# Gate stage of a streaming-encoder layer: the last 128 tokens with tokens on partitions

## The chip, the cores and the metric

The kernel runs on one core of one Trainium2 chip. The metric is the device time of one execution in microseconds (us). Times are from the program's start on the device to its end; the profile shows one execution, whose span (first to last instruction) is a little shorter than its time.

The engines are TensorE (PE; its weight loads are shown as PEld), VectorE (DVE), ScalarE (ACT), GpSimd (POOL) and SyncE (SP, which issues transfers here). PE multiplies a stationary operand (128 x 128) with a moving one (128 x up to 512 columns) and writes to PSUM, which has 8 banks of 512 columns.

## The reference, cut to what matters

One layer on 1024 tokens of width 1024: a mixer with attention, a gated MLP, and then the stage that the change touches, which takes a per-layer input embedding `p`, gates it, and adds it; a final norm closes the trunk.

```python
def rmsnorm(x, g):
    xf = x.astype(jnp.float32)
    y = xf * lax.rsqrt(jnp.mean(xf * xf, axis=-1, keepdims=True) + EPS)
    return (y * g.astype(jnp.float32)).astype(x.dtype)
...
    hn = rmsnorm(h, norm_ple_g[i])
    gate = jax.nn.sigmoid(hn @ w_ple_gate[i] + b_ple_gate[i])
    h = h + gate * (p[i] @ w_ple[i])
return rmsnorm(h, final_g)
```

`w_ple_gate` is 1024 x 1024, `p` is 1024 x 256, `w_ple` is 256 x 1024.

## The kernel before, in words

Everything is held transposed: features on the 128 partitions, tokens along the columns. The residual h is `H[d]`, d = 0 to 7 for the eight groups of 128 features, each with 1024 token columns. fp32 products are made of three products of reduced-precision halves: an operand is split into hi and lo, and `mm3` (L128) multiplies hi x hi (L130), hi x lo (L131) and lo x hi (L132). So each step over 128 features of the contraction is three matmuls.

The gate stage is a list of items (L1186). An item (d, a, b) is the feature group d for tokens a to b. Each takes `gate_mm` (8 steps over the contraction, 24 matmuls; the weights `wg` are stationary, the normalised residual `hp` is moving) and `ple_mm` (2 steps, 6 matmuls; `wp` stationary, `pt` moving). The items run in this order: eight with tokens 0 to 511, six with tokens 512 to 1023 (d = 0 to 5), and then d = 6 and 7 for tokens 512 to 767 and again for 768 to 1023. The gate products go to PSUM banks 2, 3 and 7 in turn, the ple products to 5 and 6. The loop issues the gate products of an item, then the ple products of the same item (L1205), and `gate_out` for it.

`gate_out` (L1148) is, for the second half: sigmoid on ACT (L1154), gate times ple product on DVE (L1155), residual added on DVE (L1156). Then the final norm: `Norm.add` squares the new residual on ACT (L645, L647) and adds it up over the feature groups on DVE (L649), and ACT scales the residual by the final gain (L1209).

When the last group of a token range is in, `Norm.sums` (L652) adds over the partitions with matmuls against a column of ones (L655, L657), one per 128 tokens, DVE scales (L658), and POOL raises to the power -1/2 (L659). `Norm.rows` (L661) spreads 1/rms over the partitions by a transpose on PE per 128 tokens (L663). `emit` (L1168) multiplies the residual by it on DVE (L1173) and issues the output transfers (L1174), in turn on SP's and ACT's queue. For tokens 512 to 767 the sums stand behind the gate products of the second last item and the rows in the middle of the last item's; for tokens 768 to 1023 both stand behind the last item.

PE's instructions run in the order in which the code is written (`manual_schedule`); on the other engines a scheduler orders them by their dependences and the place in the code. Each engine takes its instructions strictly one after another, and a transfer is issued by the queue of the engine that it is written on.

`hp[1]` (tokens 512 to 1023) lies in a region called B, `hp[0]`, `wg`, `pt` and `wp` in regions R0 to R4. Region 2 holds `hp[0]` (tokens 0 to 511) and is not used after item 7.

Of the kernel before, what the change touches and what calls it, by code (L numbers as in the profile page):

```python
# [6 lines left out]
F32 = mybir.dt.float32  # L7
F32R = mybir.dt.float32r
AF = mybir.ActivationFunctionType
ALU = mybir.AluOpType  # L10

P = 128
SEQ = 1024
D = 1024
KT = D // P
# [7 lines left out]
MAX_REL = 128  # L23
WINDOWS = (2, 4, 8, 16)
HIST = 16
EPS = 1e-6
BIG = 3.0e38

# [53 lines left out]


def trunk(tc, xT, pT, vecs, w_qk0, w_in, w_v, bias, counts, pool_w, w_out, w_up, w_down,
          w_gate, w_ple, out):
    nc = tc.nc
    act, dve, pe, pool, sp = nc.scalar, nc.vector, nc.tensor, nc.gpsimd, nc.sync

    with tc.tile_pool(name="sb", bufs=1) as sb, \
# [10 lines left out]
        Rs = [region(z, F32R) for z in range(5)]  # L100
        F = sb.tile([P, 15616], F32, name="F")
        ident = sb.tile([P, P], F32, name="ident")
        vec = sb.tile([P, NVEC], F32, name="vec")
        small = sb.tile([P, 80], F32, name="small")
        PS = pp.tile([P, 8, 512], F32, name="PS")
# [16 lines left out]
        def f(kb, n):  # L122
            return F[:, int(kb * KW):int(kb * KW) + n]
# [15 lines left out]
        mhalf = small[:, 0:1]  # L139
# [27 lines left out]
        qk32 = [f(38 + 4 * s, 1024) for s in range(2)]  # L167
        U = f(38, 4 * (HIST + SEQ)).rearrange("p (g t) -> p g t", g=4)
        T1 = f(54.25, 272)
# [293 lines left out]
        def pool_out(g, q, u, src, eng):  # L463

            win, n, f0 = WINDOWS[g], HIST + 256, HIST
            if q == 0:
# [105 lines left out]
        for i in range(NI + 3):  # L572
            if i >= 7:
                sums_due(i, (i - 6) // 2)
            if i < NI:
                h, t, k0, nk = keys(i)
# [43 lines left out]
        H = [f(8 + 4 * d, 1024) for d in range(KT)]  # L620
# [188 lines left out]
        for z, d in enumerate((0, 4, 1, 5, 2, 6, 3, 7)):  # L809
            k = z // 2  # L810
# [222 lines left out]
        wg = [None] * KT  # L1033
        hp = [None, None]
# [90 lines left out]
        pt = [(r(8 * k, 1024), r(8 * k + 4, 1024)) for k in range(2)]  # L1125
        wp = [(r(16 + 8 * k, 1024), r(20 + 8 * k, 1024)) for k in range(2)]
# [11 lines left out]
        def gate_mm(d, a, b, bank, middle=None):  # L1138
            ds_ = slice(d * P, (d + 1) * P)
            ts_ = slice(a % 512, a % 512 + b - a)  # L1140
            for k in range(KT):
                hi, lo = hp[a // 512][k]
                mm3(PS[:, bank, 0:b - a], wg[k][:, ds_], wg[k][:, 1024:2048][:, ds_], hi[:, ts_], lo[:, ts_],
                    k == 0, k == KT - 1)
                if k == 3 and middle:
                    middle()
# [21 lines left out]
        def emit(norm):  # L1168

            n = 1024 // (norm.nt * P)  # L1170
            for z, d in enumerate(range(0, KT, n)):
                h_ = HH[:, d:d + n, norm.ts]
                dve.tensor_tensor(h_, h_, norm.out.unsqueeze(1).to_broadcast([P, n, norm.nt * P]), ALU.mult)  # L1173
                (sp, act)[z % 2].dma_start(  # L1174
                    out[d * P:(d + n) * P, norm.ts].rearrange("(e p) t -> p e t", p=P), h_)

        zt = [f(2 * s, 512) for s in range(4)]
        acc, sq = f(52.25, 512), f(54.25, 512)
        lasts = {(0, 512): Norm(slice(0, 512), f(40, 512), [f(42, 512)], 4, 1),
                 (512, 1024): Norm(slice(512, 1024), acc, [sq], 4, 1)}  # L1180
        for z, ab in enumerate(((512, 768), (768, 1024))):
            zs = slice(256 * z, 256 * z + 256)
            lasts[ab] = Norm(slice(*ab), acc[:, zs], [sq[:, zs]], 4, z, z == 0)
            lasts[ab].n = 6
        ple_banks, gate_banks = (5, 6), (2, 3, 7)
        items = ([(d, 0, 512) for d in range(KT)] + [(d, 512, 1024) for d in range(6)]  # L1186
                 + [(d, a, a + 256) for a in (512, 768) for d in (6, 7)])

        def ended(ab):
            lasts[ab].rows()  # L1190
            emit(lasts[ab])

        for i, (d, a, b) in enumerate(items):
            gate_mm(d, a, b, gate_banks[i % 3], (lambda: ended((512, 768))) if i == 17 else None)
            if i == 0:
                continue
            if i == 16:
                lasts[512, 768].sums()
            if i == 1:
                norm_b.sums()  # L1200
            if i == 2:
                norm_b.rows(rst2[:, HS[1]])
            for z in ((0, 1) if i == 1 else (i,)):
                dz, az, bz = items[z]
                ple_mm(dz, az, bz, ple_banks[z % 2])  # L1205
                gate_out(dz, az, bz, gate_banks[z % 3], ple_banks[z % 2], zt[z % 4])
                lasts[az, bz].add(dz)
                hz = H[dz][:, az:bz]
                act.activation(hz, hz, AF.Copy, scale=vec[:, C_GL + dz:C_GL + dz + 1])  # L1209
# [12 lines left out]
def _layout(i):

    c = np.ascontiguousarray
    x = i["x"][0]
    w_in = i["w_in"][0]
    w_up = i["w_up"][0]
    d = {}
    d["xT"] = c(x.T).reshape(KT, P, SEQ)
    d["pT"] = c(i["p"][0, 0].T).reshape(2, P, SEQ)  # L1230

    def cols(v, n):
        return np.asarray(v).reshape(n, P).T

    cw = i["conv_w"][0]
    d["vecs"] = c(np.concatenate(
        [cols(i["norm_mix_g"][0], KT)] + [cols(cw[j], NF) for j in range(3)]
        + [cols(i["conv_b"][0], NF), cols(i["pool_b"][0], 4), cols(i["pool_scale"][0], 4)]
        + [cols(i[n], KT) for n in ("norm_ffn_g", "norm_ple_g", "b_ple_gate", "final_g")], axis=1))
    wt = w_in.reshape(KT, P, 16, P).transpose(2, 1, 0, 3)  # L1240
    d["w_qk0"] = c(np.concatenate([wt[4], wt[8]], axis=2)).reshape(P, KT * 2 * P)
    d["w_in"] = c(wt[:12]).reshape(12, P, D)
    d["w_v"] = c(w_in[:, 1536:].reshape(KT, P, 2, 256).transpose(2, 1, 0, 3)).reshape(2, P, KT * 256)
    ii = np.arange(P)[:, None] + 512 - np.arange(BANDT * P)[None, :]
    d["bias"] = c(i["rel_bias"][0][:, np.clip(ii, -MAX_REL, MAX_REL) + MAX_REL])
    d["counts"] = np.tile((1.0 / np.arange(1, 17)).astype(np.float32)[None, :], (P, 1))
    d["pool_w"] = c(i["pool_w"][0].transpose(1, 0, 2)).reshape(P, 512)
    d["w_out"] = c(i["w_out"][0].reshape(8, P, 2, 512).transpose(2, 0, 1, 3))
    d["w_up"] = c(w_up.reshape(KT, P, 2, NF, P).transpose(3, 2, 1, 0, 4)).reshape(NF, 2, P, D)
    d["w_down"] = c(i["w_down"][0].reshape(NF, P, D))  # L1250
    d["w_gate"] = c(i["w_ple_gate"][0].reshape(KT, P, D))
    d["w_ple"] = c(i["w_ple"][0].reshape(2, P, D))
    return d


# [15 lines left out]
```

## Time and profile before

| | us |
|---|---|
| median of 3 runs (lowest, highest) | 1139.93 (1139.84, 1141.75) |
| the profiled execution, its time | 1138.89 |
| the profiled execution, its span | 1137.1 |
| mean granted clock of TensorE | 0.997 |

How to read the rows of a profile: a row of the timeline gives the start and the length in us, the engine, the source line, the operation, output <- inputs by the program's tile names (PS is PSUM, F the working buffer that holds `H`, R and B the operand regions), the shape, and in brackets how long the engine had been idle and who released it. A "128x1 x8" row of L655 is the sums of four token tiles, each recorded as two matmuls. A row of grouped instructions ends with count, total us, mean ns, idle time before them and its releaser. A row of the windows gives a stretch, its length, the busy time of PE, PEld, DVE, ACT and POOL (with instructions started), PE's granted clock, the busy share of the transfer engines and GB/s.

### The profile page before, as it was taken

Reading aid. Unit: us, or ns where it says so; the run is one execution under the profiler, and the core shown is the slowest. Engines: PE = TensorE matmul, PEld = TensorE weight load, DVE = VectorE, ACT = ScalarE, POOL = GpSimd, SP = SyncE. Lnnn points to the kernel's source line nnn. Section 1 sums busy time; section 2 is a strip of 40 time slices with the busy share of each in tenths; the row PEclk is TensorE's granted clock in tenths of the full one; section 3 lists DMA queues with packets and bytes.
Section 4 is the critical chain, followed back from the end, with each engine's and each line's share of the span. In section 5 each row is a group of like instructions: output and inputs, shape, how many; then the busy total and the mean of one; then the engine's idle time right before and its main releaser. Section 6 shows DMA issues by size and latency. Waiting matters only on the chain.

```text
span 1137.1 us, 15326 instructions
## 1 busy us (share of the span) xinstructions
PE 1121.7 (99%) x5517; PEld 944.6 (83%) x5517; DVE 891.4 (78%) x1371; ACT 577.9 (51%) x1001; POOL 281.5 (25%) x297
## 2 busy tenths in 40 slices
PE   9999999999999999999999999999999999999996
PEld 7988998888888878888888888887888888888886
DVE  7678878779656788989898999988896688757344
ACT  8568677765554553434343434344444567545222
POOL 0013334275002213444463555333000000000000
PEclk9999999999999999999999999999999999999998
DMA  7134756534500343142635463414673564310012
GB/s 266 38 86 114 166 118 179 122 85 130 185 14 16 122 156 102 65 140 78 172 100 157 115 167 93 102 37 127 233 269 102 167 193 159 121 48 1 1 74 75
DMA packets 63340, 133.46 MB, mean 117 GB/s; under 512 B 7392, under 2 KB 9696, under 8 KB 62816
## 3 DMA queue, kind: packets, MB, share of 16 engines
q1 hardware_dynamic: 51664, 107.25, 28.5%
q0 software_dynamic: 9856, 23.07, 11.1%
q10 hardware_dynamic: 1744, 2.17, 0.5%
q8 instruction: 43, 0.70, 0.3%
q14 instruction: 33, 0.27, 0.1%
HBM read 116.73 MB, written 45.09 MB: 142 GB/s over the span
## 4 chain that ended last, share of the span: by engine, by line
PE 88%; DVE 6%; ACT 2%; issue 2%; DMA 1%; SPq 0%; DVEq 0%; POOLq 0%; POOL 0%; ACTq 0%
PE PS L130 27%; PE PS L132 27%; PE PS L131 27%; PE PS L370 2%; PE PS L387 1%; PE PS L388 1%; DVE R L136 1%; DVE B L378 1%; ACT F L356 1%; PE PS L344 1%; PE PS L345 1%; DMA F<-in_w_qk 0%; DVE F L346 0%; DMA R<-GD 0%; PE PS L353 0%
## 5 line engine op out<-in xcount | busy, mean ns | idle before, releaser
L130 PE MATMUL PS<-R,R 128*128 128x512 f32 (+1 forms) x932 | 359.7, 386 | 2.7 <-ACT R L135 1.4
L132 PE MATMUL PS<-R,R 128*128 128x512 f32 (+1 forms) x932 | 356.0, 382 | 0.0
L131 PE MATMUL PS<-R,R 128*128 128x512 f32 x868 | 338.1, 390 | 0.5 <-DVE R L231 0.5
L130 PEld LDWEIGHTS PS<-R,R 128*128 128x128 f32 x932 | 175.2, 188 | 35.5 <-ACT R L135 3.1
L132 PEld LDWEIGHTS PS<-R,R 128*128 128x128 f32 x932 | 175.1, 188 | 34.3 <-DVE R L136 0.2
L131 PEld LDWEIGHTS PS<-R,R 128*128 128x128 f32 x868 | 163.2, 188 | 33.0 <-DVE R L231 1.7
L132 PE MATMUL PS<-B 128*128 128x512 f32 x316 | 123.3, 390 | 0.1
L130 PE MATMUL PS<-B 128*128 128x512 f32 x316 | 123.3, 390 | 0.0
L131 PE MATMUL PS<-B 128*128 128x512 f32 x316 | 123.1, 390 | 0.0
L759 POOL TENSOR_TENSOR X<-X 128x512 f32<-128x512 f32 x42 | 80.2, 1912 | 122.9 <-DVE R L136 71.2
L136 DVE TENSOR_TENSOR R<-F,R 128x512 fp32r<-128x512 f32 (+1 forms) x117 | 94.0, 815 | 19.9 <-ACT R L135 19.4
L135 ACT ACTIVATE R<-F 128x512 fp32r<-128x512 f32 (+1 forms) x121 | 72.2, 613 | 72.1 <-PE PS L131 31.1
L135 ACT ACTIVATE R<-X 128x512 fp32r<-128x512 f32 x97 | 60.6, 629 | 86.0 <-PE PS L131 58.1
L136 DVE TENSOR_TENSOR R<-X,R 128x512 fp32r<-128x512 f32 x97 | 97.3, 1004 | 0.6 <-ACT R L135 0.6
L135 ACT ACTIVATE B<-F 128x512 fp32r<-128x512 f32 (+1 forms) x94 | 60.6, 646 | 70.6 <-PE PS L131 54.4
L659 POOL TENSOR_TENSOR small<-small 128x4 f32<-128x4 f32 (+1 forms) x7 | 8.1, 1158 | 336.2 <-DVE small L658 336.2
L136 DVE TENSOR_TENSOR B<-F,B 128x512 fp32r<-128x512 f32 (+1 forms) x94 | 66.6, 712 | 26.2 <-ACT B L135 25.9
L132 PEld LDWEIGHTS PS<-B 128*128 128x128 f32 x316 | 59.3, 188 | 12.9 <-DVE B L136 0.5
L131 PEld LDWEIGHTS PS<-B 128*128 128x128 f32 x316 | 59.4, 188 | 12.3
L130 PEld LDWEIGHTS PS<-B 128*128 128x128 f32 x316 | 59.4, 188 | 12.1
L131 PE MATMUL PS<-B,R 128*128 128x256 f32 (+1 forms) x208 | 64.1, 308 | 0.0
L759 POOL TENSOR_TENSOR F<-F 128x512 f32<-128x512 f32 x20 | 38.0, 1900 | 75.0 <-DVE R L136 34.9
(178 smaller groups left out, 2092.1 us busy)
## 6 DMA issues: line engine op xcount, KB each, us to landing
SD<-in_w_down POOLq DMA_DIRECT2D x54, 256.0 KB, 4.7
X<-in_w_up SPq DMA_DIRECT2D x53, 256.0 KB, 3.4
F<-SD SPq DMA_DIRECT2D x49, 256.0 KB, 2.7
R<-GD SPq DMA_DIRECT2D x44, 256.0 KB, 5.4
F<-in_w_down SPq DMA_DIRECT2D x33, 256.0 KB, 3.4
F<-in_w_up SPq DMA_DIRECT2D x32, 256.0 KB, 3.7
GD<-X SPq DMA_DIRECT2D x11, 512.0 KB, 3.3
GD<-F SPq DMA_DIRECT2D x11, 512.0 KB, 2.9
```

The source lines that it names most:

```text
L130: pe.matmul(ps, ahi, bhi, start=first, stop=False, skip_group_check=more)
L131: pe.matmul(ps, ahi, blo, start=False, stop=False, skip_group_check=more)
L132: pe.matmul(ps, alo, bhi, start=False, stop=last, skip_group_check=more)
L135: act.activation(hi, src, AF.Copy)
L136: dve.tensor_tensor(lo, src, rv(hi), ALU.subtract)
L344: pe.matmul(PS[:, 4 + z, 0:320], q, K2[:, ks], start=True, stop=False)
L345: pe.matmul(PS[:, 4 + z, 0:320], q, K1[:, ks], start=False, stop=True)
L356: act.activation(S[:, 0:n], S[:, 0:n], AF.Exp, bias=s_[:, 0:1], scale=-1.0, accum_out=s_[:, 1:2])
L370: pe.transpose(pst[:, j * P:(j + 1) * P], S[:, j * P:(j + 1) * P], ident)
L378: dve.tensor_tensor(lo, pst, rv(hi), ALU.subtract)
L387: pe.matmul(O, V[:, k, h], pt[:, 0, idx], start=n_ == 0, stop=False)
L759: pool.tensor_tensor(rawu[to], rawu[a], rawu[b], op)
```

## The change

The second half's items cover tokens 512 to 895 (`BODY` = 896): eight items of 384 columns in place of six of 512 and four of 256. The last 128 tokens are done afterwards with tokens on partitions: `hp` is stationary and `wg` is moving (`gate_tail`), `pt` is stationary and `wp` is moving (`ple_tail`). Eight transposes on PE bring the 128 tokens' residual to banks 0 and 1 (`h_t`); the ple products go to banks 5 and 6 (`ple_t`), the gate products to banks 3, 7 and 2 for 512, 256 and 256 features.

With tokens on partitions the sum of squares runs along the columns: ACT's square gives it with `accum_out`, DVE adds the three parts and POOL takes the power, for one column. Bias and gain are rows, the same on all partitions; they come in with a new input (`rows`, 128 x 2048, 1 MB) to region 2. The output of the tail is scaled half by ACT, half by DVE, and goes out token by token; the output buffer is now flat, with the tail behind the rest.

The sums of the 384 tokens stand on PE behind the first of eight steps of the first `gate_tail`, their rows behind its fourth; `emit` then works under the rest of the tail. All its four transfers are on SP's queue.

On PE the tail begins so, in the changed kernel. The first three rows are the last step of the last 384-token item's ple products (moving `pt` in R_7745, stationary `wp` in R_7746):

```order
L132 MATMUL PS<-R_7745,R_7746 128x384
L133 MATMUL PS<-R_7745,R_7746 128x384
L134 MATMUL PS<-R_7745,R_7746 128x384
L1243 MATMUL PS<-ident,F 128x128 x8
L132 MATMUL PS<-R_7746,R_7745 128x512
L133 MATMUL PS<-R_7746,R_7745 128x512
L134 MATMUL PS<-R_7746,R_7745 128x512
```

The transposes stand between the items and the tail, and the two operands of the ple products change places. (Lines of the changed kernel are two higher up to the diff's third part.)

Before, PE had the sums of tokens 512 to 767 between the gate products (B moving, R_7071 stationary) and the ple products of the second last item:

```order
L130 MATMUL PS<-B_7744,R_7071 128x256
L131 MATMUL PS<-B_7744,R_7071 128x256
L132 MATMUL PS<-B_7744,R_7071 128x256
L655 MATMUL PS<-small,F 128x1 x2
L130 MATMUL PS<-R_7745,R_7746 128x256
```

Now the sums of the 384 tokens stand behind the first step of the tail's gate products (R_6853 holds `wg` for the first four steps):

```order
L134 MATMUL PS<-R_7746,R_7745 128x512
L132 MATMUL PS<-R_6853,B_7744 128x512
L133 MATMUL PS<-R_6853,B_7744 128x512
L134 MATMUL PS<-R_6853,B_7744 128x512
L657 MATMUL PS<-small,F 128x1 x3
L132 MATMUL PS<-R_6853,B_7744 128x512
```

So what PE has between the last 384-token item and the sums is eight transposes and nine products. The last instructions of DVE before are these:

```order
L649 TENSOR_TENSOR F<-F 128x256
L1173 TENSOR_TENSOR F<-F,PS 128x4x256 x2
L1155 TENSOR_TENSOR F<-PS,F 128x256
L1156 TENSOR_TENSOR F<-F 128x256
L658 TENSOR_SCALAR small<-PS 128x2
L1173 TENSOR_TENSOR F<-F,PS 128x4x256 x2
```

And of the change, from the last 256 features on (R_8406 is region 2 with the tail's rows):

```order
L1248 TENSOR_SCALAR small<-small 128x1
L1234 TENSOR_TENSOR R_8406<-PS,R_8406 128x256
L1236 TENSOR_TENSOR R_8406<-PS,R_8406 128x256
L1237 TENSOR_TENSOR R_8406<-PS,R_8406 128x256
L1239 TENSOR_TENSOR R_8406<-R_8406 128x256
L1251 TENSOR_SCALAR small<-small 128x1
L1256 TENSOR_SCALAR R_8406<-R_8406,small 128x512
```

The scaling of four groups of 256 columns, twice, is gone from the end; one scaling of 512 columns stands there, and four additions and products on 256.

```diff
@@ emit, the norms of the second half, the items
+            dst = out[0:BODY * D].rearrange("(d t) -> d t", t=BODY)
...
-                (sp, act)[z % 2].dma_start(
-                    out[d * P:(d + n) * P, norm.ts].rearrange("(e p) t -> p e t", p=P), h_)
+                (sp, act)[z % 2 if norm.ts.start == 0 else 0].dma_start(
+                    dst[d * P:(d + n) * P, norm.ts].rearrange("(e p) t -> p e t", p=P), h_)
...
-                 (512, 1024): Norm(slice(512, 1024), acc, [sq], 4, 1)}
-        for z, ab in enumerate(((512, 768), (768, 1024))):
-            zs = slice(256 * z, 256 * z + 256)
-            lasts[ab] = Norm(slice(*ab), acc[:, zs], [sq[:, zs]], 4, z, z == 0)
-            lasts[ab].n = 6
+                 (512, BODY): Norm(slice(512, BODY), f(52.25, 512 - TAIL), [f(54.25, 512 - TAIL)], 4, 4)}
-        items = ([(d, 0, 512) for d in range(KT)] + [(d, 512, 1024) for d in range(6)]
-                 + [(d, a, a + 256) for a in (512, 768) for d in (6, 7)])
+        items = [(d, a, b) for a, b in ((0, 512), (512, BODY)) for d in range(KT)]
...
-            gate_mm(d, a, b, gate_banks[i % 3], (lambda: ended((512, 768))) if i == 17 else None)
+            gate_mm(d, a, b, gate_banks[i % 3])
-            if i == 16:
-                lasts[512, 768].sums()
...
-        lasts[768, 1024].sums()
-        ended((768, 1024))
+        Rs[2] = region(2, F32)
+        row_b, row_g, x_t, xg, o_t = [r(32 + 4 * k, D) for k in range(5)]
+        sp.dma_start(r(32, 2 * D), rows)
+        ss = small[:, 40:45]
+        wide = PS.rearrange("p a b -> p (a b)")
+        h_t, ple_t = wide[:, 0:D], wide[:, 5 * 512:5 * 512 + D]
+
+        def ple_tail(z):
+            zs = slice(z * 512, (z + 1) * 512)
+            for k in range(2):
+                mm3(ple_t[:, zs], pt[k][0][:, BODY:SEQ], pt[k][1][:, BODY:SEQ], wp[k][0][:, zs], wp[k][1][:, zs],
+                    k == 0, k == 1)
+
+        def gate_tail(z, a, b, ps, hooks=()):
+            for k in range(KT):
+                hi, lo = [t[:, BODY - 512:512] for t in hp[1][k]]
+                mm3(ps, hi, lo, wg[k][:, a:b], wg[k][:, 1024 + a:1024 + b], k == 0, k == KT - 1)
+                if k in dict(hooks):
+                    dict(hooks)[k]()
+            t = x_t[:, a:b]
+            for ins in (lambda: dve.tensor_tensor(t, ps, row_b[:, a:b], ALU.add),
+                        lambda: act.activation(t, t, AF.Sigmoid),
+                        lambda: dve.tensor_tensor(t, ple_t[:, a:b], t, ALU.mult),
+                        lambda: dve.tensor_tensor(t, h_t[:, a:b], t, ALU.add),
+                        lambda: act.activation(o_t[:, a:b], t, AF.Square, accum_out=ss[:, z:z + 1]),
+                        lambda: dve.tensor_tensor(xg[:, a:b], t, row_g[:, a:b], ALU.mult)):
+                tc.keep_in_program_order(ins())
+
+        for d in range(KT):
+            pe.transpose(h_t[:, d * P:(d + 1) * P], H[d][:, BODY:SEQ], ident)
+        ple_tail(0)
+        gate_tail(0, 0, 512, PS[:, 3], ((0, lasts[512, BODY].sums), (3, lambda: ended((512, BODY)))))
+        ple_tail(1)
+        gate_tail(1, 512, 768, PS[:, 7, 0:256])
+        dve.tensor_scalar(ss[:, 3:4], ss[:, 0:1], ss[:, 1:2], D * EPS, ALU.add, ALU.add)
+        gate_tail(2, 768, 1024, PS[:, 2, 0:256])
+        s = ss[:, 4:5]
+        dve.tensor_scalar(s, ss[:, 2:3], ss[:, 3:4], 1.0 / D, ALU.add, ALU.mult)
+        pool.tensor_tensor(s, s, mhalf, ALU.pow)
+        dst = out[BODY * D:].rearrange("(t d) -> t d", d=D)
+        act.activation(o_t[:, 0:512], xg[:, 0:512], AF.Copy, scale=s)
+        act.dma_start(dst[:, 0:512], o_t[:, 0:512])
+        dve.tensor_scalar(o_t[:, 512:D], xg[:, 512:D], s, None, ALU.mult)
+        sp.dma_start(dst[:, 512:D], o_t[:, 512:D])
```

More of the change, by code (lines that the diff above doesn't have):

```diff
@@ L25 @@
 HIST = 16
+TAIL = 128
+BODY = SEQ - TAIL
 EPS = 1e-6
@@ L84, in trunk @@
 def trunk(tc, xT, pT, vecs, w_qk0, w_in, w_v, bias, counts, pool_w, w_out, w_up, w_down,
-          w_gate, w_ple, out):
+          w_gate, w_ple, rows, out):
     nc = tc.nc
@@ L1173, in emit @@
                 dve.tensor_tensor(h_, h_, norm.out.unsqueeze(1).to_broadcast([P, n, norm.nt * P]), ALU.mult)
-                (sp, act)[z % 2].dma_start(
-                    out[d * P:(d + n) * P, norm.ts].rearrange("(e p) t -> p e t", p=P), h_)
+                (sp, act)[z % 2 if norm.ts.start == 0 else 0].dma_start(
+                    dst[d * P:(d + n) * P, norm.ts].rearrange("(e p) t -> p e t", p=P), h_)
         zt = [f(2 * s, 512) for s in range(4)]
-        acc, sq = f(52.25, 512), f(54.25, 512)
         lasts = {(0, 512): Norm(slice(0, 512), f(40, 512), [f(42, 512)], 4, 1),
-                 (512, 1024): Norm(slice(512, 1024), acc, [sq], 4, 1)}
-        for z, ab in enumerate(((512, 768), (768, 1024))):
-            zs = slice(256 * z, 256 * z + 256)
-            lasts[ab] = Norm(slice(*ab), acc[:, zs], [sq[:, zs]], 4, z, z == 0)
-            lasts[ab].n = 6
+                 (512, BODY): Norm(slice(512, BODY), f(52.25, 512 - TAIL), [f(54.25, 512 - TAIL)], 4, 4)}
         ple_banks, gate_banks = (5, 6), (2, 3, 7)
-        items = ([(d, 0, 512) for d in range(KT)] + [(d, 512, 1024) for d in range(6)]
-                 + [(d, a, a + 256) for a in (512, 768) for d in (6, 7)])
+        items = [(d, a, b) for a, b in ((0, 512), (512, BODY)) for d in range(KT)]
         def ended(ab):
@@ L1252, in _layout @@
     d["w_ple"] = c(i["w_ple"][0].reshape(2, P, D))
+    d["rows"] = np.tile(np.concatenate([i["b_ple_gate"][0], i["final_g"]])[None, :], (P, 1))
     return d
@@ L1265 @@
         args.append(nc.dram_tensor(f"in_{name}", a.shape, mybir.dt.from_np(a.dtype), kind="ExternalInput").ap())
-    out = nc.dram_tensor("out_h", (D, SEQ), F32, kind="ExternalOutput").ap()
+    out = nc.dram_tensor("out_h", (D * SEQ,), F32, kind="ExternalOutput").ap()
     with tile.TileContext(nc) as tc:
@@ L1269 @@
     r = run_bass_kernel_spmd(nc, [arrays], core_ids=[0])
-    return np.ascontiguousarray(r.results[0]["out_h"].T).reshape(1, SEQ, D)
+    o = r.results[0]["out_h"]
+    body = o[:BODY * D].reshape(D, BODY).T
+    return np.ascontiguousarray(np.concatenate([body, o[BODY * D:].reshape(TAIL, D)])).reshape(1, SEQ, D)
```

## The prediction

> **What bounds the kernel now.** I read the busy times first, then the timeline of TensorE at the last stage, then the timeline of the other engines behind its last product, and last the windows on the transfers.
>
> ```profile
> PE 1121.7 (99%) x5517; PEld 944.6 (83%) x5517; DVE 891.4 (78%) x1371; ACT 577.9 (51%) x1001; POOL 281.5 (25%) x297
> ```
>
> TensorE (PE) is busy for all but some 15 of 1137.1 us. So the time is the sum of its products, plus what follows the last of them. The change touches the second half of the gate stage alone (tokens 512 to 1023), so two pieces count: PE's run from the first product of that half to the last one, and the end behind it.
>
> ```profile
> 1067.92 0.40 PE L130 MATMUL PS<-B,R 128*128 128x512 f32 x1
> ...
> 1074.92 0.95 PE L655 MATMUL PS<-small,F 128*128 128x1 f32 x8
> 1075.73 0.48 PE L130 MATMUL PS<-B,R 128*128 128x512 f32 x1
> ...
> 1082.80 0.60 PE L663 MATMUL PS<-ident,small 128*128 128x128 f32 x4
> 1083.15 0.48 PE L130 MATMUL PS<-B,R 128*128 128x512 f32 x1
> ...
> 1111.20 0.28 PE L130 MATMUL PS<-B,R 128*128 128x256 f32 x1
> ...
> 1121.26 0.50 PE L655 MATMUL PS<-small,F 128*128 128x1 f32 x4
> 1121.62 0.36 PE L130 MATMUL PS<-R,R 128*128 128x256 f32 x1
> ...
> 1123.86 0.38 PE L663 MATMUL PS<-ident,small 128*128 128x128 f32 x2
> 1124.00 0.36 PE L130 MATMUL PS<-B,R 128*128 128x256 f32 x1
> ...
> 1126.11 0.28 PE L132 MATMUL PS<-R,R 128*128 128x256 f32 x1
> ```
>
> The durations overlap (products are pipelined), so I count from start to start. The run is 1126.11 - 1067.92 = 58.19 us. Six items of 30 products with 512 columns take 1111.20 - 1067.92 = 43.28 us; without the sums (L655: 0.81) and the 1/rms rows (L663: 0.35) that is 42.12 us, or 0.2340 us a product. Four items with 256 columns take 14.91 us; without 0.36 and 0.14 that is 14.41 us for 119 steps, or 0.1211 us. There is no gap to win back: what can be saved lies behind 1126.11.
>
> ```profile
> 1126.67 0.42 DVE L1155 TENSOR_TENSOR F<-PS,F 128x256 f32<-128x256 f32 x1
> 1127.12 0.43 DVE L1156 TENSOR_TENSOR F<-F 128x256 f32<-128x256 f32 x1
> 1127.58 0.42 ACT L647 ACTIVATE F<-F 128x256 f32<-128x256 f32 x1 [1.39 <-DVE F L1156]
> ...
> 1128.05 0.38 PE L657 MATMUL PS<-small,F 128*128 128x1 f32 x2 [1.54 <-ACT F L647]
> ...
> 1128.52 0.36 PE L657 MATMUL PS<-small,F 128*128 128x1 f32 x2
> ...
> 1128.91 0.16 DVE L658 TENSOR_SCALAR small<-PS 128x2 f32<-128x2 f32 x1 [1.37 <-PE PS L657]
> 1129.15 0.69 POOL L659 TENSOR_TENSOR small<-small 128x2 f32<-128x2 f32 x1 [6.42 <-DVE small L658]
> 1129.90 0.43 PE L663 MATMUL PS<-ident,small 128*128 128x128 f32 x2 [1.02 <-POOL small L659]
> 1130.37 2.35 DVE L1173 TENSOR_TENSOR F<-F,PS 128x1024 f32<-128x1024 f32 x2 [1.30 <-PE PS L663]
> 1132.76 0.38 ACTq L1174 DMA_DIRECT2D out_h<-F  x1
> ```
>
> This is one chain, each row released by the row above: gate times product, residual, square, sums over partitions on PE, 1/rms on POOL, its rows through PE, two scalings of 1024 elements, two transfers of 512 KB. From 1126.11 to the span's end at 1137.1 it takes 10.99 us. The last transfers by windows (columns: the stretch, its length, the busy times, PEclk, DMA share, GB/s):
>
> ```profile
> 1131.60:1132.50 0.90, 0.00 (x0) 0.00 (x0) 0.90 (x1) 0.00 (x0) 0.00 (x0) 0.50 0.00 0
> 1132.50:1134.10 1.60, 0.00 (x0) 0.00 (x0) 0.23 (x1) 0.00 (x0) 0.00 (x0) 0.50 1.00 330
> 1134.10:1135.75 1.65, 0.00 (x0) 0.00 (x0) 0.00 (x0) 0.00 (x0) 0.00 (x0) 0.50 0.91 316
> 1135.75:1137.10 1.35, 0.00 (x0) 0.00 (x0) 0.00 (x0) 0.00 (x0) 0.00 (x0) 0.50 0.00 0
> ```
>
> The first scaling ends at about 1131.6; data flows 0.90 us later, runs at some 325 GB/s for 3.25 us, and 1.35 us of completion follow.
>
> **The change part by part.**
>
> *Products.* The 180 products with 512 columns and 120 with 256 become 240 with 384, and the tail's 12 + 24 with 512 and 24 + 24 with 256. The columns are the same in number; what changes is the fixed share of each. The trace has 384 columns elsewhere, in the attention scores:
>
> ```profile
> 135.78 0.34 PE L352 MATMUL PS<-R 128*128 128x384 f32 x1
> 135.95 0.34 PE L353 MATMUL PS<-R 128*128 128x384 f32 x1
> 136.12 0.28 PE L130 MATMUL PS<-R,R 128*128 128x256 f32 x1
> ```
>
> Two steps in 0.34 us give 0.170 us; halfway between the two cadences above lies 0.1775, and that one has the operands of this stage (moving from B, stationary from R) and its refills after sums and rows. I take 0.177. So 240 x 0.177 = 42.48, 36 x 0.2340 = 8.42, 48 x 0.1211 = 5.81.
>
> *Beside the products.* The sums and rows of the first 512 tokens stay (0.81 + 0.35). The sums of three token tiles, of two records each, cost 6/8 of 0.81 = 0.61; their rows 3/4 of 0.35 = 0.26. Eight transposes of the residual (new) at the pace of the four rows cost 0.70. In all 42.48 + 8.42 + 5.81 + 0.81 + 0.35 + 0.61 + 0.26 + 0.70 = 59.44, less one step for the last start: 59.32 us, **1.13 us more** than 58.19. With 0.170 it is 0.55 us less, with 0.1775 it is 1.25 us more.
>
> *The two waits put into PE's stream.* Everything on PE is queued behind the sums at the first step and the rows at the fourth. What they wait for, from the same chain at 512 columns:
>
> ```profile
> 1110.97 0.39 PE L132 MATMUL PS<-R,R 128*128 128x512 f32 x1
> ...
> 1111.47 0.69 DVE L1155 TENSOR_TENSOR F<-PS,F 128x512 f32<-128x512 f32 x1 [4.18 <-PE PS L132]
> 1112.19 0.69 DVE L1156 TENSOR_TENSOR F<-F 128x512 f32<-128x512 f32 x1
> 1112.92 0.63 ACT L647 ACTIVATE F<-F 128x512 f32<-128x512 f32 x1 [2.22 <-DVE F L1156]
> 1113.58 0.69 DVE L649 TENSOR_TENSOR F<-F 128x512 f32<-128x512 f32 x1 [0.70 <-ACT F L647]
> ```
>
> The accumulated squares are ready 3.30 us after the last small product's start. At 384 columns the four operations are some 0.13 us shorter each: 2.8 us. PE has in that time 0.18 + 0.70 + 9 x 0.234 = 2.98 us of other work. So no wait, by a margin of 0.2 us. For the rows, DVE, POOL and hops took 1129.90 - 1128.52 = 1.4 us from the last two sums for two columns; nine products give 2.1 us; three columns on POOL add some 0.3. No wait either. What is hidden here is the whole norm of 896 - 512 tokens; if the cover fails, PE pays 1 : 1.
>
> *DVE behind it.* After the rows it scales four chunks of 768 (0.9 us each by L1173's 1.17 for 1024), then runs the chains of the tail. The scalings end some 4.1 us after the rows, the 512-column chain with two waits for ACT 3.5 us later, just as the first 256-column product ends, and each 256-column chain takes 2.7 us against 24 x 0.1211 = 2.9 us of PE. I count nothing, with 0.2 us to spare.
>
> *Output and loads.* The 1 MB of bias and gain rows is one more transfer on SP's queue, released by PE's last use of the region at about 1068; the next on that queue, the first half's outputs, follow the rows at 1083, so nothing. The four transfers of the 384 tokens go out under the last 6 us of products.
>
> *The end.* From the last product's start:
>
> ```profile
> L356 ACT ACTIVATION_READ_ACCUMULATOR F<-F,small 128x1 f32 x64 | 12.0, 187 | 0.0
> ...
> L1209 ACT ACTIVATE F<-F,vec 128x512 f32<-128x512 f32 x14 | 10.1, 725 | 0.5
> ...
> L659 POOL TENSOR_TENSOR small<-small 128x4 f32<-128x4 f32 x5 | 6.7, 1343 | 285.3 <-DVE small L658 285.3
> ...
> L361 DVE TENSOR_SCALAR F<-F,small 128x512 f32<-128x512 f32 x5 | 2.4, 484 | 0.1
> ```
>
> 0.4 to DVE; bias, product and residual on DVE (3 x 0.42), sigmoid and square on ACT (2 x 0.42), the accumulator 0.19, the last sum on DVE 0.16, POOL's power for one column 0.4 (two took 0.69, four 1.34; between 0.3 and 0.7), and about 0.3 of hops: 3.55 us. Then DVE's half of the scaling (0.48) reaches the queue at 4.05, ACT's (0.73) at 4.3. Data from 4.05 + 0.90 = 4.95; 2 x 256 KB at 325 GB/s take 1.6; 1.35 of completion: 7.9 to **8.0 us in place of 10.99**, so 3.0 less. The sums over partitions and the rows through PE are gone, and so is half of the last megabyte.
>
> **Sum**: +1.1 - 3.0 = -1.9 us. The profiled execution took 1138.89 us with 1.8 us around its span; it stands 1.04 us under the median of the three runs, 1139.93. I forecast 1139.9 - 1.9 = **1138.0 us**, 0.17% less.
>
> [...]
>
> **The rivals.**
>
> *More is won.* The 384-column products run at the 0.170 us of the attention rows, or the completion is shorter for less data. Against it: the 512-column products of this stage have the same operands from B and run at 0.2340 from their first one on. Then -0.55 - 3.0 = -3.5, with half of it -2.7: 1137.0.
>
> *The change does not do what it says: PE waits at the first step.* The margin was 0.2 us. If ACT or DVE is held by the scaling of the item before, by 1 us, PE stands 0.8 us and the DVE chains behind it shift as much: about 1139.0.
>
> *Slower.* The fixed share of a 384-column product with these operands is larger than the line between 256 and 512 says. One nanosecond is worth 0.24 us here. From 0.185 us on the end's gain is eaten; at 0.195 the change loses 2.4 us: 1142.3. A product may cost up to 512 columns' 0.2340, which would lose 12 us, but the rows at 135.78 speak clearly against it.
>
> **How the numbers follow.** Measurement tells about 0.2% from no change, 2.3 us here: faster is below 1137.65. Forecast (1138.0, own range 1137.2 to 1138.8) 0.48; more won (1137.0) 0.25; PE waits (1139.0) 0.20; slower (1142.3) 0.07. My end sum has three terms that I could not see, some 0.5 us together, and the forecast lies 0.35 us from the bound, so I give 0.08 of its chance to faster. Of the slow rival 0.01 ends within the bound. Faster 0.33, same 0.61, slower 0.06. The range leaves out the slow rival and the far end of the fast one: 1136.4 to 1139.8.
>
> **What would show it.** Right: in the second half no idle time of PE ahead of the sums and rows, last product at about 1127.2, span end 8 us later. Wrong: a 384-column cadence away from 0.177; a gap ahead of L657's or L665's instructions of the changed kernel; DVE's last chain starting over 0.6 us after the last product, which would make DVE the bound of the tail.

## The result, and the profile after

| | before | changed |
|---|---|---|
| median, us (runs) | 1139.67 (18) | 1137.88 (18) |
| ratio, 95% interval | | 0.9984 (0.9978 to 0.9991) |
| the profiled execution: time, span, us | 1138.89, 1137.1 | 1139.91, 1138.1 |
| second half of the gate stage, first to last product, us | 58.19 | 59.46 |
| last product's start to the span's end, us | 11.00 | 8.15 |

The change makes the kernel 1.79 us, or 0.16%, faster; forecast were 1.9 us and 1138.0. A repeat beside other kernels (c1, below) gave 1.52 us. The interval leaves out 1, but the gain lies below the 0.2% set as the bound of "faster" ahead of it.

The profiled execution of the changed kernel is slower than that of before, 1139.91 against 1138.89 us, though the two pieces that the change touches are together 1.58 us shorter. The changed kernel's first product of the second half starts at 1070.51 us, before's at 1067.92, and 2.4 of these 2.6 us are there by PE's 50th product, at 18.41 against 16.04 us, in a part that the change leaves alone. The windows of the changed kernel there (stretch, length, busy times of PE, PEld, DVE, ACT, POOL, PEclk, DMA share, GB/s):

```profile
10.00:15.00 5.00, 4.22 (x12) 3.12 (x13) 4.52 (x8) 5.00 (x10) 0.00 (x0) 0.74 1.05 399
12.45:15.80 3.35, 3.35 (x11) 2.67 (x10) 3.35 (x7) 3.35 (x7) 0.00 (x0) 0.50 1.04 388
```

And of before:

```profile
10.00:15.00 5.00, 4.71 (x25) 3.85 (x25) 4.86 (x8) 4.92 (x10) 0.00 (x0) 1.00 1.04 401
```

PE's timeline of the changed kernel has the pause ahead of it:

```profile
10.50 0.50 PE L132 MATMUL PS<-R,R 128*128 128x512 f32 x1 [1.84 <-ACT R L232]
```

PE stood idle for 1.84 us, and 1.9 us after the end of this pause the granted clock fell to half for 3.41 us (12.43 to 15.84). With both, 12 products started from 10 to 15 us in place of 25. Four of the changed kernel's 18 runs took 1139.88 to 1140.14 us, the others, but for one of 4431 us, 1136.90 to 1138.39; the four have a mean clock of 0.997, the others of 0.998 or 0.999. So the stages below are counted from the first product of the second half, whatever came ahead of it.

The timeline of PE, DVE and POOL in the changed kernel (start, length, engine, line, operation, and in brackets the idle time before and its releaser):

```profile
1070.51 0.34 PE L132 MATMUL PS<-B,R 128*128 128x384 f32 x1
...
1084.00 0.34 PE L132 MATMUL PS<-B,R 128*128 128x384 f32 x1
...
1085.06 0.34 PE L132 MATMUL PS<-B,R 128*128 128x384 f32 x1
...
1114.21 1.03 PE L1243 MATMUL PS<-ident,F 128*128 128x128 f32 x8
...
1115.00 0.48 PE L132 MATMUL PS<-R,R 128*128 128x512 f32 x1
...
1115.31 0.39 PE L133 MATMUL PS<-R,R 128*128 128x512 f32 x1
...
1116.22 0.56 DVE L651 TENSOR_TENSOR F<-F 128x384 f32<-128x384 f32 x1 [0.59 <-ACT F L649]
...
1116.93 0.86 PEld L657 LDWEIGHTS PS<-small,F 128*128 128x128 f32 x6
...
1117.16 0.72 PE L657 MATMUL PS<-small,F 128*128 128x1 f32 x6
1117.74 0.47 PE L132 MATMUL PS<-R,B 128*128 128x512 f32 x1
...
1118.16 0.85 POOL L661 TENSOR_TENSOR small<-small 128x3 f32<-128x3 f32 x1 [39.89 <-DVE small L660]
...
1119.93 0.49 PE L665 MATMUL PS<-ident,small 128*128 128x128 f32 x3
1120.18 0.48 PE L132 MATMUL PS<-R,B 128*128 128x512 f32 x1
...
1129.96 0.28 PE L134 MATMUL PS<-R,B 128*128 128x256 f32 x1
```

Six products with 384 columns take 1085.06 - 1084.00 = 1.06 us, 0.1767 each. The transposes take 0.79 us to the next start, and that next one 0.31 instead of 0.23, so 0.87 in all. The sums (L657) have no idle time in brackets: their operand is ready at 1116.78, 0.38 us ahead. It is their stationary operand, though, and its load (PEld) starts at 1116.93, just 0.15 us behind it. The rows (L665) wait for nothing either: POOL ends at 1119.01, 0.92 us ahead of them and 0.69 ahead of their load at 1119.70.

Behind the last product:

```profile
1129.84 0.21 DVE L1248 TENSOR_SCALAR small<-small 128x1 f32<-128x1 f32 x1
1130.28 0.42 DVE L1234 TENSOR_TENSOR R<-PS,R 128x256 f32<-128x256 f32 x1 [0.23 <-PE PS L134]
...
1131.64 0.42 DVE L1237 TENSOR_TENSOR R<-PS,R 128x256 f32<-128x256 f32 x1
...
1132.10 0.42 DVE L1239 TENSOR_TENSOR R<-R 128x256 f32<-128x256 f32 x1
...
1132.94 0.55 POOL L1252 TENSOR_TENSOR small<-small 128x1 f32<-128x1 f32 x1 [13.93 <-DVE small L1251]
1133.52 0.72 ACT L1254 ACTIVATE R<-R,small 128x512 f32<-128x512 f32 x1 [0.91 <-POOL small L1252]
...
1134.07 0.34 SPq L1257 DMA_DIRECT2D out_h<-R  x1
1134.27 0.35 ACTq L1255 DMA_DIRECT2D out_h<-R  x1
```

DVE was idle for 0.23 us ahead of the last chain: it was free just in time. The first transfer is issued 4.11 us after the last product's start. The windows behind it:

```profile
1134.07:1134.90 0.83, 0.00 (x0) 0.00 (x0) 0.00 (x0) 0.17 (x1) 0.00 (x0) 1.00 0.00 0
1134.90:1136.40 1.50, 0.00 (x0) 0.00 (x0) 0.00 (x0) 0.00 (x0) 0.00 (x0) 0.67 0.93 350
1136.40:1136.80 0.40, 0.00 (x0) 0.00 (x0) 0.00 (x0) 0.00 (x0) 0.00 (x0) 0.50 0.00 0
1136.80:1138.10 1.30, 0.00 (x0) 0.00 (x0) 0.00 (x0) 0.00 (x0) 0.00 (x0) 0.50 0.00 0
```

0.85 us pass to the first data, which then moves for 1.5 us at 350 GB/s; for 1.7 us behind it nothing moves. The two transfers land (their semaphores tell of the end) 2.1 and 2.5 us after their issue, the later one at 1136.78. From there to the span's end it is 1.34 us, in the kernel before 1.03 (1136.09 to 1137.11). The difference lies in SyncE's semaphore instructions at the program's end, which come 0.06 us apart. The profile counts those behind the last landing, first in the changed kernel and then in the one before:

```profile
L1307 SPq EVENT_SEMAPHORE  x10: 17/28/28, 1136.8 to 1138.1; - x10
```

```profile
L1267 SPq EVENT_SEMAPHORE  x5: 17/28/28, 1136.1 to 1137.1; - x5
```

Five more of them make the 0.31 us. Both kernels have eleven in all, but in the one before six come ahead of the last landing. So the end loses a tenth of its gain there.

### The profile page after: what moved, and what is told of

Its sections match the earlier page's. It is cut to its first block, busy times and chain, and to the rows that moved or that the text cites. A ratio compares the mean times of both kernels' runs of the same rounds, so it can differ in the third digit from the quotient of the medians.

```text
span 1138.1 us, 15396 instructions
## 1 busy us (share of the span) xinstructions
PE 1123.0 (99%) x5542; PEld 952.3 (84%) x5542; DVE 893.1 (78%) x1380; ACT 577.3 (51%) x1005; POOL 282.1 (25%) x297
## 4 chain that ended last, share of the span: by engine, by line
PE 90%; DVE 4%; ACT 2%; issue 2%; DMA 1%; SPq 0%; POOL 0%; POOLq 0%; ACTq 0%; DVEq 0%
PE PS L132 28%; PE PS L134 28%; PE PS L133 28%; PE PS L372 2%; PE PS L389 1%; PE PS L390 1%; ACT F L358 1%; DVE B L380 1%; DMA F<-in_w_qk 1%; DMA GD<-X 1%; PE PS L347 1%; PE PS L346 1%; DVE R L138 0%; DVE F L348 0%; PE PS L657 0%
## 5 line engine op out<-in xcount | busy, mean ns | idle before, releaser
L132 PE MATMUL PS<-R,R 128*128 128x512 f32 (+2 forms) x932 | 359.9, 386 | 4.1 <-ACT R L232 1.8
L134 PE MATMUL PS<-R,R 128*128 128x512 f32 (+2 forms) x932 | 356.3, 382 | 0.0
L133 PE MATMUL PS<-R,R 128*128 128x512 f32 (+1 forms) x868 | 338.1, 390 | 0.3 <-DVE R L233 0.3
L138 DVE TENSOR_TENSOR R<-X,R 128x512 fp32r<-128x512 f32 x97 | 99.7, 1028 | 0.6 <-ACT R L137 0.6
L133 PE MATMUL PS<-B,R 128*128 128x256 f32 (+1 forms) x192 | 57.8, 301 | 0.0
```

The lines of the kernel that those rows point to most:

```text
L132: pe.matmul(ps, ahi, bhi, start=first, stop=False, skip_group_check=more)
L133: pe.matmul(ps, ahi, blo, start=False, stop=False, skip_group_check=more)
L134: pe.matmul(ps, alo, bhi, start=False, stop=last, skip_group_check=more)
L138: dve.tensor_tensor(lo, src, rv(hi), ALU.subtract)
```

## The experiments

"Stage" is the time from the first product of the second half to the last; "end" is from that last start to the span's end. The changed kernel has 59.46 and 8.15 us (the pieces are taken from the unrounded starts, so that a hundredth may differ from the rows).

**c1: the changed kernel again.**

> The changed kernel once more, beside the next one on the same chip. As before: median 1137.9, stage 59.46, end 8.15 us.

Median 1137.57 us of 11 runs beside 1139.09 of 16 of the kernel before, ratio 0.9986 (0.9977 to 0.9995); stage 59.46, end 8.15 us. The profile of this execution has the clock at 1.0 at the start, and a span of 1135.6 us. Its second half starts at 1068.02 us, not at 1070.51. So the gain repeats, and not every execution of the changed kernel has the late start.

**a2: no cover for the two waits.** Cover is the work that PE has between the last 384-token item and the instruction that has to wait.

```diff
+        lasts[512, BODY].sums()
+        ended((512, BODY))
         for d in range(KT):
             pe.transpose(h_t[:, d * P:(d + 1) * P], H[d][:, BODY:SEQ], ident)
         ple_tail(0)
-        gate_tail(0, 0, 512, PS[:, 3], ((0, lasts[512, BODY].sums), (3, lambda: ended((512, BODY)))))
+        gate_tail(0, 0, 512, PS[:, 3])
```

> The sums and the 1/rms rows of the 384 tokens stand behind the last 384-token item, ahead of the transposes, instead of behind the first and the fourth step of the tail's gate products. Theory (PE covers two waits): without cover PE waits for the accumulated squares, 2.57 us from its last small product to the end of L651 in the changed kernel less one step, so 2.3 to 2.6 us, and 1.3 to 1.6 us more for DVE, POOL and the rows' operand, so the stage's 59.45 us become 63.0 to 63.7; the end behind the last product stays at 8.1 us. Rival (the scheduler or other work fills the gap, the order is of no weight): 59.5.

Its timeline of PE, and its windows:

```profile
1114.99 1.32 PE L657 MATMUL PS<-small,F 128*128 128x1 f32 x6 [2.46 <-DVE F L651]
1117.49 0.90 PE L665 MATMUL PS<-ident,small 128*128 128x128 f32 x3 [1.18 <-POOL small L661]
1118.19 1.91 PE L1245 MATMUL PS<-ident,F 128*128 128x128 f32 x8
```

```profile
1115.00:1117.00 2.00, 1.31 (x6) 1.22 (x6) 0.16 (x1) 0.00 (x0) 0.41 (x1) 0.54 0.03 8
1117.00:1119.00 2.00, 1.51 (x7) 1.51 (x8) 0.57 (x1) 0.00 (x0) 0.44 (x1) 0.50 0.00 0
1119.00:1121.00 2.00, 2.00 (x9) 1.81 (x8) 2.00 (x3) 0.00 (x0) 0.00 (x0) 0.50 0.33 117
```

The first wait is as expected, 2.46 us, and the second a little shorter, 1.18; but the stage is 66.10 us, 6.64 more than with cover and 2.4 above the expected range. The other 3.0 us go with the clock: it stands at 0.5 for 6.83 us from the first wait on, and the transposes take 1.91 us instead of 1.03. The end is 8.15 us. So the cover is real, and what it keeps off is not priced by the wait alone.

**b1: half the cover.** The sums stand directly behind the transposes, the rows behind the tail's second gate step.

> The sums of the 384 tokens stand directly behind the eight transposes, ahead of the tail's ple products, and the rows behind the second step of the tail's gate products. In a2 PE stood idle 2.46 us ahead of the sums and 1.18 us ahead of the rows, and the stage grew by 6.6 us, not by their 3.6: the granted clock was 0.5 for 6.83 us behind it. Here the transposes cover 0.87 of the 2.46, so PE idles 1.6 us, and the rows have 12 products ahead of them and wait for nothing. Theory A (a short wait costs its own length, since pauses of 1.4 to 1.65 us elsewhere in these runs left the clock at 1.0): the stage is 59.45 + 1.6 = 61.0 to 61.2 us. Theory B (this pause halves the clock too, for one stretch of 3.41 us): 62.4 to 62.9. The end behind the last product stays 8.1 to 8.2.

Timeline and windows:

```profile
1115.04 0.83 PE L657 MATMUL PS<-small,F 128*128 128x1 f32 x6 [1.59 <-DVE F L651]
```

```profile
1115.00:1116.80 1.80, 1.76 (x11) 1.59 (x12) 0.16 (x1) 0.04 (x1) 0.65 (x1) 0.99 0.00 0
1116.80:1118.50 1.70, 1.70 (x6) 1.31 (x5) 0.00 (x0) 0.00 (x0) 0.20 (x1) 0.50 0.00 0
1118.50:1120.20 1.70, 1.70 (x6) 1.21 (x5) 0.00 (x0) 0.00 (x0) 0.00 (x0) 0.50 0.00 0
```

Stage 62.88 us, theory B: 3.42 more, of which 1.59 us are the wait and 1.7 us come from 3.41 us at half clock. In those 3.4 us the 512-column products start every 0.43 us. Theory A falls: a pause of 1.59 us here had the clock halved, while pauses of 1.58 and 1.65 us earlier in the runs (at about 794.8 and 794.7 us in b1 and a2) had not, and one of 1.88 us in b2 at 794 had.

**a3: sums and rows three steps later.**

```diff
-        gate_tail(0, 0, 512, PS[:, 3], ((0, lasts[512, BODY].sums), (3, lambda: ended((512, BODY)))))
+        gate_tail(0, 0, 512, PS[:, 3], ((3, lasts[512, BODY].sums), (6, lambda: ended((512, BODY)))))
```

> The sums stand behind the fourth step and the rows behind the seventh step of the tail's first gate products (first and fourth in the changed kernel). Theory (DVE is 0.23 us from being the bound of the tail: it becomes free 0.23 us before the last product can be used): the scalings start 9 products = 2.1 us later, every chain behind them as well, so the end from the last product's start grows from 8.14 us by about 1.9 us to 10.0. Rival (DVE has slack, since the 256-column chains are shorter than their products): the end stays within 0.3 us of 8.14. The stage on PE stays at 59.45 under both.

The timeline about its last product:

```profile
1127.51 0.28 PE L134 MATMUL PS<-R,B 128*128 128x256 f32 x1
...
1129.51 0.41 DVE L1234 TENSOR_TENSOR R<-PS,R 128x256 f32<-128x256 f32 x1
```

Stage 59.46, end 9.83 us: DVE takes up the last product 2.00 us after its start, in place of 0.32, and no releaser stands in its brackets: it was busy until then. 9 products or some 2.1 us later cost 1.68, so DVE's slack was some 0.4 us, a little over the 0.23 that the idle time shows. The place of the sums is bounded on both sides, by PE's wait and by DVE.

**a4: the tail in the old layout.**

```diff
-        items = [(d, a, b) for a, b in ((0, 512), (512, BODY)) for d in range(KT)]
+        items = [(d, a, b) for a, b in ((0, 512), (512, BODY), (BODY, SEQ)) for d in range(KT)]
...
-            gate_mm(d, a, b, gate_banks[i % 3])
+            gate_mm(d, a, b, gate_banks[i % 3], (lambda: ended((512, BODY))) if i == 19 else None)
+            if i == 17:
+                lasts[512, BODY].sums()
...
+        lasts[BODY, SEQ].sums()
+        ended((BODY, SEQ))
```

The tail's own code is gone.

> The last 128 tokens are done like the 384 before them, with features on partitions: eight items of 128 columns, the sums of the 384 tokens behind the gate products of the second of them, the rows in the middle of the fourth, and at the end sums, rows and one scaling of 8 x 128 columns with one transfer of 512 KB. So the split 512 + 384 + 128 stays and only the tail's layout goes. Theory 1 (a product's fixed share is a line through 512, 384 and 256 columns, 0.2333, 0.1767, 0.1172): 128 columns take 0.059, 240 of them 14.2 us, and PE's stage is 59.2 to 59.7 us, no loss by narrow products. Theory 2 (a 128-column product has a floor, as the transposes' 0.10 us a step): 24 us, so the stage takes 69. The end behind the last product: 0.3 to DVE, five operations of some 0.25, sums 0.4, 0.2, POOL 0.55, rows 0.35, one scaling 1.2, 0.4 to the queue and 0.9 + 1.6 + 1.35 of transfer, with hops 8.3 to 9.0 us, against 8.14.

Its timeline of PE and of the last issue:

```profile
1116.80 0.28 PE L132 MATMUL PS<-B,R 128*128 128x128 f32 x1
...
1117.47 0.78 PE L657 MATMUL PS<-small,F 128*128 128x1 f32 x6
...
1139.09 0.27 PE L134 MATMUL PS<-R,R 128*128 128x128 f32 x1
...
1143.75 0.37 SPq L1179 DMA_DIRECT2D out_h<-F  x1
```

Six products with 128 columns take 0.67 us, 0.112 each: nearly as much as one with 256 (0.117). Theory 2 holds for this width; the stage is 71.31 us and not its 69, since it took 0.10 us a product. The end is 8.81, the whole 1149.70 us in one run. At 0.112 us in place of half of 0.117, the 128 tokens can be split off only because the weights move in their place, 512 and 256 columns wide. The end gains just 0.66 us from the layout; most of the end's gain comes from the smaller last piece. Counted to the last landing, so without the instructions at the program's end, it is 9.98 us before, 7.84 here and 6.82 in the changed kernel: 2.14 from the smaller piece and 1.02 from the layout.

**b2: the last output twice.** The two transfers of 256 KB are issued once more, to a scratch buffer.

> Behind the two output transfers of 256 KB each the kernel writes the same 512 KB once more, to a scratch buffer, on the same two queues. Theory (the end is bound by bytes, as the forecast's sum has it): 512 KB more at the 394 GB/s of the changed kernel's last full stretch, 1.3 us, so the end behind the last product grows from 8.14 to 9.3 to 9.6 us. Rival (a transfer's fixed share and its completion bound the end, and bytes are hidden in it): 8.1 to 8.5.

The windows behind its first issue, at 1133.51 us, 4.12 us after the last product at 1129.39:

```profile
1134.40:1135.20 0.80, 0.00 (x0) 0.00 (x0) 0.00 (x0) 0.00 (x0) 0.00 (x0) 0.50 1.03 376
1135.20:1136.20 1.00, 0.00 (x0) 0.00 (x0) 0.00 (x0) 0.00 (x0) 0.00 (x0) 0.50 1.03 387
1136.20:1137.30 1.10, 0.00 (x0) 0.00 (x0) 0.00 (x0) 0.00 (x0) 0.00 (x0) 0.50 0.87 315
1137.30:1138.80 1.50, 0.00 (x0) 0.00 (x0) 0.00 (x0) 0.00 (x0) 0.00 (x0) 0.50 0.00 0
```

End 9.44 us, stage 59.46. The added bytes cost 1.29 us at the end. Data moves from 1134.34 to 1137.26, for 2.92 us at 359 GB/s in place of 1.50 us at 350, and from the last landing to the span's end it is 0.13 us less. Bytes bound the end, on top of 0.85 us ahead of them and 1.6 to 1.7 behind.

**c3: two queues for the 384 tokens' output**, as the first half has it.

> The four output transfers of the 384 tokens go out in turn on SP's and ACT's queue, as the ones of the first half do, instead of all on SP's. Theory (an issue on ACT's queue makes ACT wait for the scaling ahead of it, and the sigmoid of the tail's first 512 columns stands behind it): the 512-column sigmoid starts up to 0.5 us later, but the last chain is 256 columns on and DVE, not ACT, is what it waits for, so the end stays 8.1 to 8.4 us and the stage 59.4 to 59.5. Rival (the queue is of weight): an end of 8.8 us or more.

Stage 59.46, end 8.17 us, and the 512-column sigmoid starts 5.32 us ahead of the last product as in the changed kernel. The choice of SP's queue alone is of no weight.

**a1: region B moved by 32 bytes.**

```diff
-        small = sb.tile([P, 80], F32, name="small")
+        small = sb.tile([P, 88], F32, name="small")
```

> One tile of the kernel is made 32 bytes longer, so that region B starts at a multiple of 64 bytes like the regions R (it started 32 bytes past one). In the changed kernel a 512-column product with both operands in R, or both in B, starts every 0.2267 us, one with an operand from each some 0.231 to 0.234, and a 384-column product of the gate stage (B moving, R stationary) every 0.1767. Theory (the 32 bytes between the two operands cost the 4 to 6 ns): the 384-column cadence falls to about 0.171, the 512-column cadence of the tail's gate products to 0.2267, and the gate stage's second half, 59.45 us from its first product to its last, becomes 57.8 to 58.3; with the attention's and first products' steps the whole kernel gains 2 to 4 us. Rival (it is the change between regions, or refill after a break, whatever the address): no change, within 0.2 us in that stage.

Its timeline of PE:

```profile
1067.62 0.34 PE L132 MATMUL PS<-B,R 128*128 128x384 f32 x1
...
1126.89 0.28 PE L134 MATMUL PS<-R,B 128*128 128x256 f32 x1
```

Stage 59.27 us, 0.19 less: the theory's 1.2 to 1.6 falls, and the rival's "within 0.2" holds. Median 1136.82 us of 9 runs, ratio to before 0.9976 (0.9966 to 0.9986), which overlaps with the changed kernel's interval. Why the first half's 512-column products take 0.2267 us and the tail's 0.230 to 0.234 stays open. The regions alone are not it: the tail's ple products have both operands in R, as the first half's have, and start every 0.230 to 0.232 us.

**b3: the bias in PSUM.**

```diff
+            if i >= 13:
+                ca, cb = ((0, 512), (512, 768), (768, 1024))[i - 13]
+                act.activation(PS[:, gate_banks[i % 3], 0:cb - ca], row_b[:, ca:cb], AF.Copy)
...
-                mm3(ps, hi, lo, wg[k][:, a:b], wg[k][:, 1024 + a:1024 + b], k == 0, k == KT - 1)
+                mm3(ps, hi, lo, wg[k][:, a:b], wg[k][:, 1024 + a:1024 + b], False, k == KT - 1, True)
...
-            for ins in (lambda: dve.tensor_tensor(t, ps, row_b[:, a:b], ALU.add),
-                        lambda: act.activation(t, t, AF.Sigmoid),
+            for ins in (lambda: act.activation(t, ps, AF.Sigmoid),
```

The rows are loaded behind item 9; the last scaling is split 640 to 384, and a1's line is in.

> The bias row is put into PSUM by ACT ahead of the tail's gate products (behind items 13, 14 and 15), the products add onto it, and the sigmoid reads PSUM: the additions on DVE go. The last scaling is split 640 columns on DVE, 384 on ACT; region B starts at a multiple of 64 bytes as in a1. Theory: one operation of 0.46 us with its hop leaves the end's chain, and the two halves of the scaling end together, 0.1 us earlier: the end behind the last product 8.14 - 0.46 - 0.1 = 7.5 to 7.7 us; the stage 59.2 to 59.3 as in a1; the median 0.6 us under a1's, 1136.2. Rival (DVE with its scalings of the 384 tokens, or the copies on ACT, hold the tail): end of 8.1 or more, or idle time of PE ahead of the tail's gate products.

Its timeline at the end:

```profile
1127.09 0.28 PE L134 MATMUL PS<-R,B 128*128 128x256 f32 x1
1127.41 0.38 ACT L1237 ACTIVATE R<-PS 128x256 f32<-128x256 f32 x1 [0.99 <-PE PS L134]
...
1130.78 0.34 SPq L1259 DMA_DIRECT2D out_h<-R  x1
```

Median 1136.12 us of 4 runs, ratio 0.9962 (0.9948 to 0.9977); stage 59.27, end 7.76 us, just above the 7.5 to 7.7 expected. The first issue comes 3.69 us after the last product, 0.42 earlier than in the changed kernel: the addition is gone. The other split of the scaling brought nothing: from that issue to the span's end it is 4.07 us (4.05 before it).

**b4 and c2: no transposes on PE either.**

```diff
+            if 10 <= i <= 13:
+                for d in (2 * i - 20, 2 * i - 19):
+                    dve.transpose(h_b[:, d * P:(d + 1) * P], H[d][:, BODY:SEQ])
+            if i == 13:
+                hb, ht = [t.rearrange("p (d j t) -> p d j t", d=KT, j=4) for t in (h_b, h_t)]
+                for a_ in range(4):
+                    for j in range(4):
+                        sp.dma_start(ht[32 * j:32 * j + 32, :, a_, :], hb[32 * a_:32 * a_ + 32, :, j, :])
...
-        for d in range(KT):
-            pe.transpose(h_t[:, d * P:(d + 1) * P], H[d][:, BODY:SEQ], ident)
...
-        gate_tail(0, 0, 512, PS[:, 3], ((0, lasts[512, BODY].sums), (3, lambda: ended((512, BODY)))))
+        gate_tail(0, 0, 512, PS[:, 3], ((1, lasts[512, BODY].sums), (4, lambda: ended((512, BODY)))))
```

> As b3, and the residual of the 128 tokens is turned by DVE in blocks of 32 x 32 while PE works on the 384-token items, and brought into place by 16 transfers within SBUF: PE's eight transposes go. Their cover ahead of the sums goes too, so sums and rows stand behind the second and the fifth step of the tail's gate products. Theory (0.87 us of PE's stream go, sums keep a margin of 0.38 - 0.87 + 0.70 = 0.2 us): the stage 58.3 to 58.5 us, the end 7.5 to 7.7, the median 1135.3. Rival (the sums are late, or DVE's scalings now end behind the last product): idle time ahead of the sums, or an end of 8 us or more, and no gain against b3.

> The kernel of b4 once more. By the profiles its stage is 1.02 us and its end 0.39 us shorter than the changed kernel's, so its median is 1.4 us lower, 1136.5 or less; if the profiles mislead (other runs start differently), the difference is under 0.5 us.

The timeline of b4:

```profile
1114.22 0.72 PE L657 MATMUL PS<-small,F 128*128 128x1 f32 x6
...
1126.43 0.29 PE L134 MATMUL PS<-R,B 128*128 128x256 f32 x1
...
1130.11 0.34 SPq L1266 DMA_DIRECT2D out_h<-R  x1
```

No idle time ahead of the sums. Stage 58.44 us, 0.83 less than b3: the transposes' price on PE; end 7.76. Medians 1135.96 us (1135.3 expected; 5 runs; ratio 0.9967, 0.9951 to 0.9982) and, in c2, 1135.39 us (6 runs; stage 58.43; ratio 0.9965, 0.9953 to 0.9977), 2.2 us under the changed kernel on the same chip, of which the profiles' stage and end show 1.4; 0.44 more lie ahead of the stage in these two profiles, and the rest stays open. Against b3 the medians of b4 tell no difference; only the profiles do.

## Why the prediction was right

*The sum.* Forecast 59.32 and 8.0 us, measured 59.46 and 8.15, so -1.58 us by the profiles in place of -1.9; the medians say -1.79 and -1.52. The likeliest case came in, and its place between "faster" and "same" too. That the numbers lie so close is in part luck. In the stage, the transposes were taken 0.17 us too low and the 48 products with 256 columns 0.18 too high: they start every (1129.96 - 1124.45) / 47 = 0.1172 us, not 0.1211. And 1138.0 was counted from a median of three runs, 0.26 us above that of the 18.

*Products.* 0.177 us with 384 columns held: 0.1767 in steady stretches, and the eight items with the first half's sums and rows take 1114.21 - 1070.51 = 43.70 us, against 42.48 + 0.81 + 0.35 = 43.64 forecast. The rival "more is won" by 0.170 is refuted here, as is the "slower" one by 0.195. What it feared shows further down: a4's products with 128 columns take 0.112 us, nearly the 0.117 of 256.

*Transposes* were under-sized: 0.87 by the starts and 0.83 by b3 against b4, not 0.70. Their own pace is slower than that of the four rows from which it was taken (0.79 us for eight), and the slower step behind them (0.08) was left out.

*The two waits.* No wait, as forecast; the margin at the sums was 0.38, not 0.2 us, because the last item's chain was 2.75 us long, from its last product's start at 1114.03, and the transposes longer. By the weight load it was 0.15 us. In b4 the load does come late, 0.16 us ahead of its product in place of 0.23 (operand ready at 1114.00, load at 1114.06), and PE still shows no idle time. a2 shows that the cover is needed, and a3 that DVE's limit is as near on the other side. The rival "PE waits" was priced 1 : 1, and in two runs that was too little: 1.6 us of waiting cost 3.4 in b1, and 3.64 cost 6.64 in a2. For the 0.8 us that it named the price may stand: PE pauses for 0.78 us up to 413.12 in the profile of before and for 0.83 us up to 415.48 in that of the changed kernel, with the clock at 1.0 from 410 to 416 us in both.

*The end.* Chain to the first issue 4.11 us, forecast 4.05. POOL took 0.55 for one column (0.4 taken, 0.3 to 0.7 given). Behind the issue one term was too small and two were too large: the data came after 0.85 us (0.90), moved for 1.5 (1.6, at 325 GB/s instead of 350), and nothing moved in the last 1.7 (1.35). The prediction carried these 1.35 us over from the kernel before; what it left out are the five more semaphore instructions, 0.31 us. b2 confirms that the bytes count in full.

*Landing, and reads from PSUM.* From the first issue to the last landing it is 2.71 us, 2.1 and 2.5 for the two transfers by themselves; the 4.03 us to the span's end hold the program's last instructions too. While data moves, it moves at 350 GB/s in the changed kernel and at 359 in b2, above the prediction's 325. The 0.42 us that it took for each of the end's operations on DVE held, whether they read PSUM or not: L1237 with PSUM and L1239 without both take 0.42 us.

## What to carry to other kernels

The last piece of this kernel pays its chain (4.11 us to the first issue) and its bytes (1.29 us for 512 KB more in b2) in full, so make such a piece small; but along the moving side a product with 128 columns took 0.112 us here, against 0.117 with 256, and then the operands have to change places. Work that waits for another engine goes behind as much of the busy engine's stream as the chain lasts (2.75 us here), and no further, since the engine that follows has its own slack (some 0.4 us of DVE's here); both margins can be read from starts and idle times before anything is run. Price a wait on TensorE with the clock that it may lose (1.59 us of waiting cost 3.42 in b1), and compare stage by stage from a common start when executions start unevenly (1070.51 and 1068.02 us in two profiles of the changed kernel).

## What the runs showed of the hardware

TensorE's granted clock was halved for 3.41 us after a pause of 1.59 us in b1, of 1.84 at the start of the changed kernel's profiled execution and of 1.88 in b2 at 794 us, and for 6.83 us after the pauses of 2.46 and 1.18 us in a2; not after 1.58 us (b1, at about 794.8 us) and 1.65 us (a2, at about 794.7 us). So it isn't the length alone that decided. The clock falls 1.7 us after the pause's end in b1 and 0.2 after it in a2, so its falls do not follow the pauses at one distance. In these profiles two of them lie a whole number of steps of 3.41 us apart, the length of the half-clock stretch. In b1 it falls at 1116.78 us and, behind PE's last product, again at 1133.85: 17.07 us or 5 steps of 3.41. In a2 it falls at 1115.16 and 1139.05, 7 steps apart, in b2 at 796.46 and 1134.38, 99 steps of 3.413, and in the changed kernel's profile at 12.43 and 1135.41, 329 steps of 3.413. An estimate that carries the steps on through each run puts b1's 1.59 us within one step (1113.37 to 1116.78), and cuts the 1.58 us that left the clock alone at 795.93 into 1.12 and 0.46; but it puts a2's 1.65 us, which left the clock alone too, within one step as well (794.31 to 797.72). So where a pause lies in a step may count, but that it decides is not shown; nor does any run here isolate how much idle time is enough.

In a4 a product with 128 columns (B moving, R stationary) takes 0.112 us, hardly less than one with 256 in the changed kernel's tail (R moving, B stationary) at 0.117.
